# Layer B of a two-layer decoder: the norms of queries and keys, one chain for two token blocks in place of one for each

## The chip, the cores and the metric

One NeuronCore of a Trainium2 chip runs the whole program in one launch. The metric is device time in microseconds (us), and lower is better. The names of the engines in this document are those of the profile: PE is TensorE, DVE is VectorE, ACT is ScalarE, POOL is GpSimd, SP issues most of the DMAs.

## What is computed

The input x has 1024 tokens of 1024 columns, in float32; 16 learned meta tokens are put ahead of them. Layer A (stick-breaking attention and an MLP) comes first. Layer B has differential attention with 8 heads. Of each head it needs two queries and two keys of 64 columns and one value of 128 columns. Each query and key row is normalised and turned by position before the scores:

```python
kk = kv[..., :DIFF_HEADS * 2 * DIFF_QK_DIM].reshape(B, T, DIFF_HEADS, 2, DIFF_QK_DIM)
k1 = apply_partial_rope(rmsnorm(kk[..., 0, :], kv_k_norm_g[0]), cos, sin)
k2 = apply_partial_rope(rmsnorm(kk[..., 1, :], kv_k_norm_g[1]), cos, sin)
...
qq = (hn @ b_w_q[j]).reshape(B, T, DIFF_HEADS, 2, DIFF_QK_DIM)
q1 = apply_partial_rope(rmsnorm(qq[..., 0, :], b_q_norm_g[j, 0]), cos, sin)
q2 = apply_partial_rope(rmsnorm(qq[..., 1, :], b_q_norm_g[j, 1]), cos, sin)
o = differential_attention(q1, q2, k1, k2, vv, lam)
```

`rmsnorm(x, g)` is `x * rsqrt(mean(x * x) + EPS) * g`, here over 64 columns: one number for each token and each of the four rows (two queries, two keys).

## The kernel before

**Stages.** The program runs layer A's attention, its MLP, layer B's attention (the stretch from about 1399 to 2004 us of the span) and layer B's MLP. The change touches layer B's attention alone.

**Items of a head.** Tokens are handled in 8 blocks of 128 (b = 1 to 8); b = 0 is the 16 meta tokens. For head h and block b, `item(b)` makes the projection: 24 matmuls of 384 columns into a PSUM tile `bpj` (two buffers, tag `pj`), of which columns 0 to 255 are the four query and key rows of 64 and the last 128 are the value. ACT and DVE turn the value into the two halves `bv`. `rope_block` then takes the query and key part. ACT writes it to `raw` and its squares to `bsq`; DVE sums the squares to four numbers in `ss`, and scales them and adds EPS; `rsqrt` takes Ln on ACT, and `newton` takes Exp on ACT and then three small instructions on DVE (`na`, `na`, `ny`). Next DVE multiplies `raw` by `ny` into `kn`, POOL multiplies by the gains and does the rotation (six to ten instructions), ACT makes the first half of `hl` and DVE the second. For block 1 the two key rows of the meta tokens join: n = 6 columns in place of 4.

**Transposes.** `rope_stack(b)` turns `hl` by four PE transposes into a PSUM tile `bq`, which ACT copies into the head's `q` and `k` tiles. For heads 1 to 7 that tile has the tag `pj` too, so `bpj` and `bq` share two buffers, and they get them in the order of the program. `hl` and `kn` have two buffers each.

**Attention.** `b_unit(h, g)` makes scores (`sc_b`) of 256 queries against all keys so far, their maximum (`mxb`, DVE), exponentials (`eb`, `wb`, ACT) and the weighted difference (`wb`, DVE). `b_unit_av` transposes it (`ptb`, evacuated to `wtb` by ACT and DVE) and multiplies by the values (`avb`).

**What sets the order.** The code lists the items and transposes of head h + 1 in a stream that is fed between the pieces of head h's attention; the transpose of block b is listed DEFER = 3 blocks behind its projection. A scheduler then fixes the order of each engine's instructions when the program is built. Which engine does a copy (`evac`, `scopy`) is decided by running sums of estimated costs in `load`. On the chip each engine takes its instructions in that fixed order.

**Weights.** The first item of a head also loads its weights (`bws`, three buffers), scales them on POOL, and splits them on ACT (`bwh`) and DVE (`bwl`, 128x384, eight of them). They have nine buffers for eight pieces, so most of a head's splits wait until the last projection of the head ahead of it has read its own.

Of the kernel before, what the change touches and what calls it, by code (L numbers as in the profile page):

```python
# [8 lines left out]
F32 = mybir.dt.float32  # L9
F32R = mybir.dt.float32r  # L10
BF16 = mybir.dt.bfloat16
AF = mybir.ActivationFunctionType
ALU = mybir.AluOpType
# [65 lines left out]
def kernel(ctx: ExitStack, tc: tile.TileContext, inp, out):  # L79
# [23 lines left out]
    def act(o, i, func, **kw):  # L103
        load["a"] += 64 + 0.86 * fsize(o) + (93 if "bias" in kw else 0)
        nc.scalar.activation(out=o, in_=i, func=func, **kw)  # L105
# [5 lines left out]
    def tt(o, a, b, op):  # L111
        load["v"] += 60 + 1.04 * fsize(o)
        nc.vector.tensor_tensor(out=o, in0=a, in1=b, op=op)  # L113
# [1111 lines left out]
    with ExitStack() as st:  # L1225
# [28 lines left out]
        def rsqrt(v, n, tag, tg="n"):  # L1254

            y = sp.tile([P, 8], F32, tag=f"{tg}y", bufs=2, name=f"ny{tag}")[:, :n]
            a = sp.tile([P, 8], F32, tag=f"{tg}a", bufs=2, name=f"na{tag}")[:, :n]
            act(y, v, AF.Ln)
            newton(y, v, a)
            return y  # L1260

        def rope_block(h, b, ps, tm):

            tag = f"{h}_{b}"
            n = 6 if b == 1 else 4
            ss = sp.tile([P, 8], F32, tag="ss", bufs=2, name=f"ss{tag}")
            sq = sp.tile([P, 4, HD], F32, tag="sq", bufs=1, name=f"bsq{tag}")
            kn = sp.tile([P, 6, HD], F32, tag="kn", bufs=2, name=f"kn{tag}")
            raw = sp.tile([P, 4, HD], F32, tag="raw", bufs=2, name=f"raw{tag}")
# [3 lines left out]
            nc.vector.tensor_reduce(out=ss[:, 0:4], in_=sq, axis=AX.X, op=ALU.add)  # L1273
            if b == 1:
                nc.vector.memset(ss[:, 4:6], 1.0)
                nc.gpsimd.memset(kn[:, 4:6], 1.0)
                for m in range(2):
                    act(sq[:NM, m], tm[:, m * HD:(m + 1) * HD], AF.Square, accum_out=ss[:NM, 4 + m:5 + m])
            nc.vector.tensor_scalar(out=ss[:, :n], in0=ss[:, :n], scalar1=1.0 / HD, scalar2=EPS, op0=ALU.mult, op1=ALU.add)
            y = rsqrt(ss[:, :n], n, tag)  # L1280
            tt(kn[:, 0:4], raw, y[:, 0:4, None].to_broadcast([P, 4, HD]), ALU.mult)
            if b == 1:
                tt(kn[:NM, 4:6], tm[:, 0:P].rearrange("p (m d) -> p m d", d=HD), y[:NM, 4:6, None].to_broadcast([NM, 2, HD]), ALU.mult)
                ptt(kn[:, 4:6], kn[:, 4:6], gqk[:, 2:4], ALU.mult)
# [34 lines left out]
        def b_items(h):  # L1319
# [26 lines left out]
            def item(b):  # L1346
# [25 lines left out]
                st_[b] = rope_block(h, b, ps, st_["tm"])  # L1372
# [254 lines left out]
```

## Time and profile before

| what | us |
|---|---|
| median of 3 runs | 2743.18 |
| lowest and highest of them | 2738.76, 2744.81 |
| the profiled execution, its own time | 2740.28 |
| span of that execution, first to last instruction | 2738.5 |
| PE busy in it | 2613.1 |
| DVE busy | 1987.0 |
| ACT busy | 1508.1 |
| POOL busy | 318.1 |

The profile is of one execution, whose time lies 2.9 us below the median of the runs, and 1.8 us above its own span. Busy times are unions of an engine's instructions, so that two that overlap count once.

### The profile page before, as it was taken

Reading aid. Unit: us, or ns where it says so; the run is one execution under the profiler, and the core shown is the slowest. Engines: PE = TensorE matmul, PEld = TensorE weight load, DVE = VectorE, ACT = ScalarE, POOL = GpSimd, SP = SyncE. Lnnn points to the kernel's source line nnn. Section 1 sums busy time; section 2 is a strip of 40 time slices with the busy share of each in tenths; the row PEclk is TensorE's granted clock in tenths of the full one; section 3 lists DMA queues with packets and bytes.
Section 4 is the critical chain, followed back from the end, with each engine's and each line's share of the span. In section 5 each row is a group of like instructions: output and inputs, shape, how many; then the busy total and the mean of one; then the engine's idle time right before and its main releaser. Section 6 shows DMA issues by size and latency. Waiting matters only on the chain.

```text
span 2738.5 us, 49906 instructions
## 1 busy us (share of the span) xinstructions
PE 2613.1 (95%) x18271; PEld 2469.2 (90%) x18271; DVE 1987.0 (73%) x4009; ACT 1508.1 (55%) x3545; POOL 318.1 (12%) x708
## 2 busy tenths in 40 slices
PE   7999999989899999999989999999898999999999
PEld 7899898869899999999989899999897999987787
DVE  6998888897775665865767788888768666557645
ACT  4566666675355555344546667677545555544443
POOL 2211111000000000000024344443100000000000
PEclk9999999999999999999999999999999999999999
DMA  7333332345334446843431122223352444486343
GB/s 208 98 85 83 84 83 77 103 131 149 99 129 140 151 146 223 319 118 101 135 88 44 40 55 55 55 55 104 118 172 69 156 142 155 154 317 225 93 110 121
DMA packets 298711, 341.76 MB, mean 125 GB/s; under 512 B 32538, under 2 KB 209347, under 8 KB 298467
## 3 DMA queue, kind: packets, MB, share of 16 engines
q1 hardware_dynamic: 289106, 334.32, 39.4%
q10 hardware_dynamic: 9360, 4.26, 0.6%
q8 instruction: 144, 2.36, 0.4%
q14 instruction: 101, 0.82, 0.1%
HBM read 206.99 MB, written 97.28 MB: 111 GB/s over the span
## 4 chain that ended last, share of the span: by engine, by line
PE 74%; DVE 11%; DMA 4%; ACT 3%; issue 2%; POOL 1%; SPq 1%; DVEq 0%; ACTq 0%; POOLq 0%
PE mia L159 12%; PE mib L159 11%; PE moa L159 11%; PE mob L159 9%; PE bpj L159 8%; PE pj L159 6%; PE opb L159 2%; PE sc_b L159 2%; DVE kp L498 2%; PE av L159 2%; PE avb L159 2%; PE sc L159 2%; PE pt L162 1%; PE opa L159 1%; DMA bb<-u_d 1%
## 5 line engine op out<-in xcount | busy, mean ns | idle before, releaser
L159 PE MATMUL moa<-wba,waa 128*128 128x260 f32 x2688 | 325.3, 284 | 0.4 <-DVE wba L113 0.4
L159 PEld LDWEIGHTS moa<-wba,waa 128*128 128x128 f32 x2688 | 324.7, 189 | 0.6 <-DVE wba L113 0.6
L159 PE MATMUL mob<-wab,wbb 128*128 128x512 f32 x1344 | 313.8, 394 | 4.5 <-DVE hqb L113 2.8
L159 PEld LDWEIGHTS mob<-wab,wbb 128*128 128x128 f32 x1344 | 251.7, 188 | 65.6 <-issue 3.9
L159 PE MATMUL pj<-xa,wh 128*128 128x400 f32 (+2 forms) x1152 | 291.2, 332 | 6.1 <-DVE rsa L668 5.8
L159 PE MATMUL bpj<-bwh,xb 128*128 128x384 f32 x1024 | 285.7, 347 | 8.9 <-ACT k L99 5.4
L159 PEld LDWEIGHTS pj<-xa,wh 128*128 128x128 f32 x1152 | 202.2, 192 | 7.7 <-POOL ws L121 6.1
L159 PEld LDWEIGHTS bpj<-bwh,xb 128*128 128x128 f32 x1024 | 187.7, 190 | 13.7 <-ACT k L99 8.5
L498 DVE TENSOR_TENSOR_SCAN kp<-kp 128x144 f32<-128x144 f32 (+7 forms) x128 | 184.6, 1447 | 18.2 <-ACT kp L105 17.4
L159 PE MATMUL pj<-xa,wl 128*128 128x384 f32 (+2 forms) x576 | 189.8, 329 | 0.1
L159 PE MATMUL bpj<-bwl,xb 128*128 128x384 f32 x512 | 174.1, 340 | 0.0
L1338 POOL TENSOR_SCALAR bws<-bws,gains 128x128 f32<-128x128 f32 (+1 forms) x128 | 64.7, 511 | 832.8 <-DVE accx L113 776.9
L105 ACT ACTIVATE w<-sc,rsa 128x392 f32<-128x392 f32 (+4 forms) x224 | 121.2, 543 | 42.2 <-PE sc L159 40.4
L105 ACT ACTIVATE kp<-sc,rsa 128x392 f32<-128x392 f32 (+4 forms) x224 | 120.1, 538 | 15.6 <-DVE w L113 15.6
L1396 DVE TENSOR_REDUCE mxb<-sc_b 128x1 f32<-128x144 f32 (+6 forms) x224 | 109.3, 502 | 15.6 <-PE sc_b L159 14.0
L99 ACT CAST wt<-pt 128x512 fp32r<-128x512 f32 (+1 forms) x160 | 84.5, 546 | 61.2 <-PE av L159 45.3
L162 PE MATMUL pt<-cst,w 128*128 128x128 f32 x576 | 96.5, 279 | 21.0 <-DVE w L113 9.0
L113 DVE TENSOR_TENSOR wt<-pt,wt 128x512 fp32r<-128x512 f32 (+1 forms) x160 | 98.2, 628 | 19.7 <-ACT wt L99 18.9
L113 DVE TENSOR_TENSOR w<-w,kp 128x143 f32<-128x143 f32 (+7 forms) x128 | 110.9, 872 | 2.0
L159 PE MATMUL av<-wt,v 128*128 128x256 f32 (+1 forms) x640 | 105.3, 288 | 6.5 <-DVE wt L113 5.6
L159 PEld LDWEIGHTS pj<-xa,wl 128*128 128x128 f32 x576 | 110.0, 191 | 0.6 <-DVE wl L113 0.4
L159 PEld LDWEIGHTS av<-wt,v 128*128 128x128 f32 x640 | 90.2, 192 | 10.6 <-DVE wt L113 7.2
(484 smaller groups left out, 7417.3 us busy)
## 6 DMA issues: line engine op xcount, KB each, us to landing
ba<-u_d SPq DMA_DIRECT2D x112, 260.0 KB, 2.8
bb<-u_d SPq DMA_DIRECT2D x112, 256.0 KB, 2.7
mwsa<-in_mlp_w_in_dram SPq DMA_DIRECT2D x32, 512.0 KB, 3.9
mwsb<-in_mlp_w_in_dram SPq DMA_DIRECT2D x32, 512.0 KB, 3.9
o_d<-oh SPq DMA_DIRECT2D x52, 256.0 KB, 2.5
ws<-in_a_w_qkv_dram SPq DMA_DIRECT2D x24, 512.0 KB, 4.2
qb<-q SPq DMA_DIRECT2D x128, 64.0 KB, 2.0
a12a<-in_mlp_w_out_dram SPq DMA_DIRECT2D x16, 512.0 KB, 8.0
```

The lines of the kernel that those rows point to most:

```text
L99: nc.scalar.copy(out=o, in_=i)
L105: nc.scalar.activation(out=o, in_=i, func=func, **kw)
L113: nc.vector.tensor_tensor(out=o, in0=a, in1=b, op=op)
L159: return nc.tensor.matmul(o, lhsT=l, rhs=r, start=start, stop=stop, **kw)
L162: return nc.tensor.transpose(out=o, in_=i, identity=ident)
L498: nc.vector.tensor_tensor_scan(out=rv, data0=rv, data1=rv, initial=1.0, op0=ALU.mult, op1=ALU.bypass)
L1338: nc.gpsimd.tensor_scalar(out=ws[:, s], in0=ws[:, s], scalar1=gains[:, gc + k:gc + k + 1], scalar2=1.0, op0=ALU.mult, op1=ALU.mult)
L1396: nc.vector.tensor_reduce(out=mx[:, j:j + 1], in_=ps[:, 0], axis=AX.X, op=ALU.max, negate=True)
```

## The change

`rope_block` of an odd block now stops after its sum of squares and returns nothing; it leaves `ss` and `raw` in `prs`. `rope_block` of the even block behind it puts its own four sums beside them, and one chain (scale, Ln, Exp, `na`, `na`, `ny`) is run on 8 columns, or 10 for blocks 1 and 2 with the meta tokens' two. Then the new function `rope` is called twice, for the odd block and for the even one: it holds the multiplication by `ny`, the rotation and the making of `hl`, as they were. `raw` gets four buffers in place of two. The number of matmuls stays as it was; the built program has 125 DVE and 66 ACT instructions fewer.

```diff
@@ -1253,8 +1253,8 @@
 
         def rsqrt(v, n, tag, tg="n"):
 
-            y = sp.tile([P, 8], F32, tag=f"{tg}y", bufs=2, name=f"ny{tag}")[:, :n]
-            a = sp.tile([P, 8], F32, tag=f"{tg}a", bufs=2, name=f"na{tag}")[:, :n]
+            y = sp.tile([P, 10], F32, tag=f"{tg}y", bufs=2, name=f"ny{tag}")[:, :n]
+            a = sp.tile([P, 10], F32, tag=f"{tg}a", bufs=2, name=f"na{tag}")[:, :n]
             act(y, v, AF.Ln)
             newton(y, v, a)
             return y
@@ -1262,25 +1262,42 @@
         def rope_block(h, b, ps, tm):
 
             tag = f"{h}_{b}"
-            n = 6 if b == 1 else 4
-            ss = sp.tile([P, 8], F32, tag="ss", bufs=2, name=f"ss{tag}")
+            odd = b % 2
+            if odd:
+                prs["ss"] = sp.tile([P, 10], F32, tag="ss", bufs=2, name=f"ss{tag}")
+            ss = prs["ss"]
             sq = sp.tile([P, 4, HD], F32, tag="sq", bufs=1, name=f"bsq{tag}")
-            kn = sp.tile([P, 6, HD], F32, tag="kn", bufs=2, name=f"kn{tag}")
-            raw = sp.tile([P, 4, HD], F32, tag="raw", bufs=2, name=f"raw{tag}")
+            raw = sp.tile([P, 4, HD], F32, tag="raw", bufs=4, name=f"raw{tag}")
             evac(raw.rearrange("p m d -> p (m d)"), ps[:, 0:2 * P], scale=rsx[:, b:b + 1])
             act(sq, raw, AF.Square)
             load["v"] += 60 + 1.04 * 4 * HD
-            nc.vector.tensor_reduce(out=ss[:, 0:4], in_=sq, axis=AX.X, op=ALU.add)
+            o = 2 if odd else 6
+            nc.vector.tensor_reduce(out=ss[:, o:o + 4], in_=sq, axis=AX.X, op=ALU.add)
             if b == 1:
-                nc.vector.memset(ss[:, 4:6], 1.0)
+                nc.vector.memset(ss[:, 0:2], 1.0)
+                for m in range(2):
+                    act(sq[:NM, m], tm[:, m * HD:(m + 1) * HD], AF.Square, accum_out=ss[:NM, m:m + 1])
+            if odd:
+                prs["raw"] = raw
+                return []
+            v = ss[:, 0 if b == 2 else 2:10]
+            n = v.shape[1]
+            nc.vector.tensor_scalar(out=v, in0=v, scalar1=1.0 / HD, scalar2=EPS, op0=ALU.mult, op1=ALU.add)
+            y = rsqrt(v, n, tag)
+            return [rope(h, b - 1, prs["raw"], y[:, n - 8:n - 4], y[:, 0:2], tm), rope(h, b, raw, y[:, n - 4:n], None, tm)]
+
+        prs = {}
+
+        def rope(h, b, raw, y, ym, tm):
+
+            tag = f"{h}_{b}"
+            n = 6 if b == 1 else 4
+            kn = sp.tile([P, 6, HD], F32, tag="kn", bufs=2, name=f"kn{tag}")
+            if b == 1:
                 nc.gpsimd.memset(kn[:, 4:6], 1.0)
-                for m in range(2):
-                    act(sq[:NM, m], tm[:, m * HD:(m + 1) * HD], AF.Square, accum_out=ss[:NM, 4 + m:5 + m])
-            nc.vector.tensor_scalar(out=ss[:, :n], in0=ss[:, :n], scalar1=1.0 / HD, scalar2=EPS, op0=ALU.mult, op1=ALU.add)
-            y = rsqrt(ss[:, :n], n, tag)
-            tt(kn[:, 0:4], raw, y[:, 0:4, None].to_broadcast([P, 4, HD]), ALU.mult)
+            tt(kn[:, 0:4], raw, y[:, :, None].to_broadcast([P, 4, HD]), ALU.mult)
             if b == 1:
-                tt(kn[:NM, 4:6], tm[:, 0:P].rearrange("p (m d) -> p m d", d=HD), y[:NM, 4:6, None].to_broadcast([NM, 2, HD]), ALU.mult)
+                tt(kn[:NM, 4:6], tm[:, 0:P].rearrange("p (m d) -> p m d", d=HD), ym[:NM, :, None].to_broadcast([NM, 2, HD]), ALU.mult)
                 ptt(kn[:, 4:6], kn[:, 4:6], gqk[:, 2:4], ALU.mult)
             ptt(kn[:, 0:4], kn[:, 0:4], gqk, ALU.mult)
             t0 = 0 if b == 1 else b
@@ -1369,7 +1386,8 @@
                 r = rsx[:, b:b + 1]
                 acopy(d["v"][:, b, 0, :], ps[:, 2 * P:], scale=r)
                 stt(d["v"][:, b, 1, :], ps[:, 2 * P:], r, f(d["v"][:, b, 0, :]), ALU.mult, ALU.subtract)
-                st_[b] = rope_block(h, b, ps, st_["tm"])
+                for x, hl in zip((b - 1, b), rope_block(h, b, ps, st_["tm"])):
+                    st_[x] = hl
 
             return item, lambda b: rope_stack(d, h, b, st_[b])
```

Where instructions stand now. In the names below the first number is the head and the second the block (`ny5_2`: head 5, block 2), for `sc_b`, `mxb` and `avb` the second is the unit g; the last number is the buffer's own.

VectorE at the start of head 5, before: the chain of block 1 ends here, and that of block 2 begins.

```order
L113 TENSOR_TENSOR na5_1_22455<-ny5_1_22454 128x6
L1396 TENSOR_REDUCE mxb4_2_0_22324<-sc_b4_2_0_1_328_22341 128x1
L117 SCALAR_TENSOR_TENSOR na5_1_22455<-na5_1_22455,ss5_1_22442 128x6
L1396 TENSOR_REDUCE mxb4_2_1_22355<-sc_b4_2_1_0_0_22356 128x1
L1398 TENSOR_TENSOR mxb4_2_0_22324<-mxb4_2_0_22324 128x1
L117 SCALAR_TENSOR_TENSOR ny5_1_22454<-na5_1_22455,ny5_1_22454 128x6
L1273 TENSOR_REDUCE ss5_2_22516<-bsq5_2_22517 128x4
L109 COPY os3_21553<-psq3_3_22411 128x2
L113 TENSOR_TENSOR kn5_1_22444<-raw5_1_22445,ny5_1_22454 128x256
L113 TENSOR_TENSOR kn5_1_22444<-tm5_22306,ny5_1_22454 16x128
L1279 TENSOR_SCALAR ss5_2_22516<-ss5_2_22516 128x4
```

The same place of the changed kernel, on VectorE:

```order
L113 TENSOR_TENSOR na5_2_22312<-ny5_2_22311 128x10
L1416 TENSOR_TENSOR mxb4_2_1_22175<-mxb4_2_1_22175 128x1
L113 TENSOR_TENSOR wtb4_1_1_22457<-ptb4_1_1_22453,wtb4_1_1_22457 128x384
L117 SCALAR_TENSOR_TENSOR na5_2_22312<-na5_2_22312,ss5_1_22262 128x10
L117 SCALAR_TENSOR_TENSOR ny5_2_22311<-na5_2_22312,ny5_2_22311 128x10
L113 TENSOR_TENSOR kn5_1_22318<-raw5_1_22264,ny5_2_22311 128x256
L113 TENSOR_TENSOR kn5_1_22318<-tm5_22126,ny5_2_22311 16x128
L113 TENSOR_TENSOR kn5_2_22341<-raw5_2_22306,ny5_2_22311 128x256
L1427 TENSOR_TENSOR s04_20945<-mxb4_2_1_22175 128x1
L117 SCALAR_TENSOR_TENSOR bv5_22027<-bpj5_3_22498,rsx_81,bv5_22027 128x128
```

One chain of 10 columns (`128x10`) now serves both blocks, and the two multiplications into `kn5_1` and `kn5_2` stand one behind the other, with the meta tokens' between them.

VectorE at the end of head 5, before: block 8's chain ends, and block 7, whose chain stood further up, gets its `hl`.

```order
L113 TENSOR_TENSOR na5_8_23256<-ny5_8_23255 128x4
L117 SCALAR_TENSOR_TENSOR wb5_1_23120<-eb5_1_0_23134,mxb5_1_0_23121,wb5_1_23120 128x400
L117 SCALAR_TENSOR_TENSOR na5_8_23256<-na5_8_23256,ss5_8_23247 128x4
L1409 TENSOR_TENSOR s05_22208<-mxb5_1_1_23139 128x1
L117 SCALAR_TENSOR_TENSOR ny5_8_23255<-na5_8_23256,ny5_8_23255 128x4
L113 TENSOR_TENSOR hl5_7_23107<-kn5_7_23082,hl5_7_23107 128x4x64
L113 TENSOR_TENSOR kn5_8_23249<-raw5_8_23250,ny5_8_23255 128x256
```

The same chain of the changed kernel, on VectorE:

```order
L113 TENSOR_TENSOR na5_8_23023<-ny5_8_23022 128x8
L1427 TENSOR_TENSOR s05_22028<-mxb5_1_1_22908 128x1
L113 TENSOR_TENSOR bwl6_7_23187<-bws6_7_23182,bwh6_7_23186 128x384
L117 SCALAR_TENSOR_TENSOR na5_8_23023<-na5_8_23023,ss5_7_22873 128x8
L117 SCALAR_TENSOR_TENSOR ny5_8_23022<-na5_8_23023,ny5_8_23022 128x8
L113 TENSOR_TENSOR kn5_7_23029<-raw5_7_22875,ny5_8_23022 128x256
L113 TENSOR_TENSOR kn5_8_23045<-raw5_8_23017,ny5_8_23022 128x256
```

Block 7's multiplication into `kn5_7` now waits for block 8's chain, and its `hl5_7` comes 19 rows behind the last of these. Counted over the whole order, from the instruction that reads block 8's projection (`bv`) to `hl` of block 7 there are, for heads 1 to 6, 30, 25, 34, 40, 34, 37 DVE rows before, and 62, 47, 45, 52, 51, 42 now. On TensorE, from the last matmul of block 8's projection to the first transpose of block 7, there are 89, 120, 110, 120, 110, 117 matmuls before, and 127, 125, 129, 131, 124, 115 now.

TensorE where head 1 ends and head 2 begins, before: the transposes of head 1's block 7 (`bq1_7`) and the first projection of head 2 (`bpj2_1`).

```order
L159 MATMUL bpj2_0_19013<-bwl2_6_18998,xm_17056 48x256
L159 MATMUL bpj2_0_19013<-bwh2_7_19007,xm_17056 48x256
L159 MATMUL avb0_3_18710<-wtb0_3_3_18815,bv0_17068 128x256 x2
L159 MATMUL avb0_3_18710<-wtb0_3_3_18815,bv0_17068 128x128 x3
L159 MATMUL psq0_2_18841<-ones_66,osqb0_2_18523 128x2 x2
L159 MATMUL sc_b1_1_1_1_0_18693<-k1_17772,q1_1_17774 128x264
L159 MATMUL sc_b1_1_1_1_0_18693<-k1_17772,qbb1_1_18657 128x264
L162 MATMUL bq1_7_19058<-idr_62,hl1_7_18647 128x128 x4
L159 MATMUL bpj2_0_19013<-bwl2_7_19008,xm_17056 48x256
L159 MATMUL bpj2_1_19065<-bwh2_0_18937,xb0_16177 128x384
```

The same place of the changed kernel, on TensorE:

```order
L159 MATMUL sc_b1_2_0_1_328_18801<-idb_64 128x128
L159 MATMUL sc_b1_2_1_0_0_18816<-k1_17736,q1_2_17739 128x392
L159 MATMUL sc_b1_2_1_0_0_18816<-k1_17736,qbb1_2_18780 128x392
L159 MATMUL avb1_0_18846<-wtb1_0_0_18851,bv1_17741 128x256 x2
L159 MATMUL avb1_0_18846<-wtb1_0_0_18851,bv1_17741 128x128 x3
L159 MATMUL psq0_3_18982<-ones_66,osqb0_3_18767 128x2 x2
L159 MATMUL avb1_0_18846<-bzm0_17053,bvm1_17055 128x256 x2
L162 MATMUL ptb1_1_0_19117<-cst_60,wb1_1_18573 128x128 x4
L162 MATMUL bq1_7_18986<-idr_62,hl1_7_18713 128x128 x4
L159 MATMUL bpj2_1_18993<-bwh2_0_18865,xb0_16177 128x384
```

The transposes still stand directly ahead of head 2's projections. But the matmuls that stand there without a projection between them are now 79 (all of attention, or `bq1_7`), where the longest such run in the middle of the stage was 41 before.

## Rows read from the trace of the kernel before

**Rows 1.** The page, part 1: busy us, share, instructions by engine.
```profile
PE 2613.1 (95%) x18271; PEld 2469.2 (90%) x18271; DVE 1987.0 (73%) x4009; ACT 1508.1 (55%) x3545; POOL 318.1 (12%) x708
```

**Rows 2.** Busy time by stretch: heading, and the whole stage.
```profile
core 0: us, PE busy (x) PEld busy (x) DVE busy (x) ACT busy (x) POOL busy (x), PEclk, DMA share, GB/s
1399.00:2004.00 605.00, 572.42 (x3797) 535.64 (x3796) 475.00 (x1583) 395.31 (x1331) 226.76 (x636) 0.98 0.24 68
```

**Rows 3.** Busy time by stretch: first and last of six boundaries, and sum.
```profile
1518.00:1550.20 32.20, 30.36 (x205) 27.59 (x204) 26.57 (x92) 22.33 (x78) 15.91 (x43) 1.00 0.23 61
...
1860.00:1893.20 33.20, 31.87 (x224) 29.90 (x225) 31.29 (x104) 24.40 (x86) 15.08 (x41) 1.00 0.27 73
sum 185.10, PE 179.08 PEld 168.21 DVE 168.69 ACT 135.45 POOL 95.31; mean PE 29.85 PEld 28.03 DVE 28.12 ACT 22.58 POOL 15.89
```

**Rows 4.** Busy time by stretch: sum of six middles between them.
```profile
sum 231.80, PE 223.82 PEld 209.52 DVE 175.80 ACT 154.30 POOL 71.97; mean PE 37.30 PEld 34.92 DVE 29.30 ACT 25.72 POOL 12.00
```

**Rows 5.** Waits of TensorE, 1446 to 1940: total us, times, longest.
```profile
PE bpj L159 <- ACT k L99: 6.5, 15, 1.1
PE avb L159 <- DVE wtb L113: 2.4, 5, 0.8
PE sc_b L159 <- ACT eb L105: 2.1, 3, 0.9
```

**Rows 6.** Groups by line and shape, 1399 to 2004: the merged instructions.
```profile
L105 ACT ACTIVATE ny<-ss 128x4 f32<-128x4 f32 x56 | 12.0, 214 | 13.7 <-DVE ss L1279 13.7
...
L1279 DVE TENSOR_SCALAR ss<-ss 128x4 f32<-128x4 f32 x56 | 11.1, 198 | 0.8
...
L113 DVE TENSOR_TENSOR na<-ny 128x4 f32<-128x4 f32 x56 | 9.7, 174 | 4.3 <-ACT ny L105 3.9
...
L117 DVE SCALAR_TENSOR_TENSOR na<-na,ss 128x4 f32<-128x4 f32 x56 | 9.2, 163 | 0.6
...
L117 DVE SCALAR_TENSOR_TENSOR ny<-na,ny 128x4 f32<-128x4 f32 x56 | 8.8, 158 | 0.8
```

**Rows 7.** VectorE in order of time, in a boundary: start, us.
```profile
1754.34 0.15 DVE L113 TENSOR_TENSOR nao<-nyo 128x8 f32<-128x8 f32 x1
1754.45 0.16 DVE L117 SCALAR_TENSOR_TENSOR na<-na,ss 128x4 f32<-128x4 f32 x1
1754.53 0.16 DVE L117 SCALAR_TENSOR_TENSOR nao<-nao,os 128x8 f32<-128x8 f32 x1
1754.65 0.16 DVE L117 SCALAR_TENSOR_TENSOR ny<-na,ny 128x4 f32<-128x4 f32 x1
1754.73 0.26 DVE L117 SCALAR_TENSOR_TENSOR nyo<-nao,nyo 128x8 f32<-128x8 f32 x1
1754.91 0.41 DVE L113 TENSOR_TENSOR kn<-raw,ny 128x256 f32<-128x256 f32 x1
1755.25 0.55 DVE L1396 TENSOR_REDUCE mxb<-sc_b 128x1 f32<-128x392 f32 x1
```

**Rows 8.** VectorE in order of time, head 0, block 1.
```profile
1424.74 0.17 DVE L117 SCALAR_TENSOR_TENSOR na<-na,ss 128x6 f32<-128x6 f32 x1
1424.94 0.17 DVE L117 SCALAR_TENSOR_TENSOR ny<-na,ny 128x6 f32<-128x6 f32 x1
```

**Rows 9.** VectorE in order of time: block 7, heads 1, 4, 5.
```profile
1527.64 0.41 DVE L113 TENSOR_TENSOR hl<-kn,hl 128x256 fp32r<-128x256 f32 x1
...
1737.79 0.63 DVE L113 TENSOR_TENSOR hl<-kn,hl 128x256 fp32r<-128x256 f32 x1
...
1806.41 0.43 DVE L113 TENSOR_TENSOR hl<-kn,hl 128x256 fp32r<-128x256 f32 x1 [0.99 <-ACT hl L144]
```

**Rows 10.** TensorE in order of time: the transposes of those blocks.
```profile
1528.33 0.46 PE L162 MATMUL bq<-idr,hl 128*128 128x128 f32 x4
...
1741.33 0.51 PE L162 MATMUL bq<-idr,hl 128*128 128x128 f32 x4
...
1807.71 0.54 PE L162 MATMUL bq<-idr,hl 128*128 128x128 f32 x4
```

## The prediction

> **What bounds the kernel now.** I read the page first. PE is busy for 95% of the span, DVE for 73%, ACT for 55% [rows 1]. The change removes no matmul, so the question is where in layer B's attention, the 605 us from 1399 to 2004, PE is held up by DVE or ACT. Over that stage PE is busy for 572.4 us and DVE for 475.0 [rows 2], which looks like PE's stage. Cut in pieces it is two things. I took the time at which DVE finishes `bv` of block 8 of a head and of block 3 of the next, for heads 1 to 6. In these six boundaries, 185.1 us together, DVE is busy for 168.7, or 91% [rows 3]; this is where the next head's eight `bwl` come on top. In the six middles between them, 231.8 us, DVE is busy for 175.8, or 76%, and PE for 223.8, or 97% [rows 4]. So what leaves DVE can be worth something in the boundaries, and is hidden by PE's projections in the middles. The waits of PE from 1446 to 1940 us give the ceiling of what can be won where PE shows as idle: the three largest are 6.5 us for `k` from ACT, 2.4 for `wtb` from DVE and 2.1 for `eb` from ACT [rows 5]. None is for the tiles that the change touches.
>
> **The change part by part.**
>
> *Merged instructions.* 64 chains become 32. On DVE that is 32 x 4 = 128 instructions fewer (the order shows 125, as a few copies change engine), on ACT 64 fewer (66 in the order). Their mean durations are 198, 174, 163 and 158 ns on DVE and some 210 on ACT [rows 6], so the busy times should fall by up to 32 x 0.69 = 22 us on DVE and 32 x 0.42 = 13.5 on ACT. Columns hardly cost: 4 to 10 of them are far below what such an instruction takes. But the time that matters is from start to start. In a boundary, with an independent instruction behind it, `na` holds DVE for 1754.53 - 1754.45 = 0.08 us and `ny` for the same [rows 7]. With the next of its own chain directly behind it, it holds DVE for 1424.94 - 1424.74 = 0.20 us [rows 8]. Counted over the order, 82 chain instructions stand in the six boundaries now and 46 after, 36 fewer; pairs of dependents that are direct neighbours there rise from 10 to 16, since fewer chains leave less to put between. The gain in the boundaries is then 36 x 0.10 - 6 x 0.12 = 2.9 us. The bounds are 36 x 0.08 - 0.7 = 2.2 and, by full durations, 36 x 0.17 = 6.2. I take 2.9, since rows 7 are from a boundary and rows 6 count overlaps. In the middles and in head 0 I take 0: PE covers it.
>
> The Trainium skill, page "Perfetto Trace Analysis", section "Optimizing Scalar/DVE Operations", puts DVE's overhead per instruction at about 60 ns on SBUF and says that grouping helps if the engine is saturated. By that figure the boundaries would give 36 x 0.06 = 2.2 us (an estimate from that page), the lower of my bounds; rows 7 agree with it nearly.
>
> *Moved work.* The odd block's multiplication into `kn`, its rotation on POOL (a gain product, four products, two sums; more for block 1), `hl` on ACT and DVE, and four transposes now come behind the even block's squares. On DVE, 3 `kn` and 3 `hl` fewer stand in the six boundaries (21 each before, 18 now); they move to the middles. At 1755.25 - 1754.91 = 0.34 us each [rows 7] that is 2.0 us, between 0 (if the next boundary pays) and 6 x 0.43 = 2.6. On POOL two rotations now run one after the other; POOL is busy for 95.3 of 185.1 us there [rows 3], so half of it is free, and I cost this at 0. If POOL were late, `hl` would be, and its price is that of the next paragraph. SP's queue gets its q copies for the scores later by a place or two; they are read two blocks on. 0.
>
> *A later block 7.* The transposes of block b stand three items behind its projection. For blocks 1, 3 and 5 the odd block loses one item of three, some 24 matmuls. Block 7 is tight already: in head 1 its `hl` ends at 1528.05 and PE takes it at 1528.33, in head 4 1738.42 and 1741.33, in head 5 1806.84 and 1807.71, so 0.3, 2.9 and 0.9 us to spare [rows 9, 10] (hl of block 7 is the (8h + 7)th on DVE). Behind it on PE stand the next head's projections, which share its PSUM buffers. In the changed order `hl` of block 7 stands 32, 22, 11, 12, 17 and 5 DVE rows further behind block 8's `bv` in heads 1 to 6, at some 0.33 us a row (33.2 us for 104 [rows 3]): 10.6, 7.3, 3.6, 4.0, 5.6 and 1.7 us. PE comes to it 38, 5, 19, 11, 14 and -2 matmuls later, at 33.2/224 = 0.15 us: 5.7, 0.8, 2.9, 1.7, 2.1, -0.3. With head 4's 2.9 us to spare where I have no row, PE would wait 4.6 us in head 1, 3.6 in head 2, 2.6 in head 5 and 0 elsewhere: up to 11 us. Most of it comes back: the rows that come in between are the next attention's scores done early, and over the six boundaries DVE's rows fall from 567 to 519. I take 1.0, of 0 to 11.
>
> *ACT.* The waits for `k` are for ACT, which loses 13.5 of 395 us [rows 2]: 3% of 6.5 us, so 0.2; at most half of it, 3.2.
>
> *The sum.* -2.9 - 2.0 + 1.0 - 0.2 = -4.1 us. The profiled execution took 2740.3 itself (a span of 2738.5 and 1.8 around it) and would be at 2736.2. It lies 2.9 below the median of the runs, 2743.2, so a median of runs should be near **2739 us**. That is 0.15% less; 0.2%, or 5.5 us, is about what a measurement of this kernel can tell from no change.
>
> **The rivals.**
>
> *Faster beyond that.* The boundaries are so full that DVE's durations count whole: 6.2 + 2.6, and ACT gives the 3.2: -12, so 2731. For it: DVE at 91% there; the last boundary took 33.2 us for 31.3 us of DVE work [rows 3]. Against it: PE is at 97% in the same stretches (179.1 of 185.1), so that its own matmuls follow close behind. It decides from 1.4 us more than the sum.
>
> *Slower.* Block 7 late, with nothing given back: PE stops at `bq` ahead of the next head's projections. With 11 in place of 1.0 the sum is +6, so 2749; with POOL's two rotations in a row late by another 0.5 us in seven heads, 2753. For it: 0.3 us to spare in head 1, and 79 matmuls without a projection between them there. Against it: DVE has 48 rows less to do over the six boundaries. It decides from some 10 us of new waits of PE for `hl`. The Trainium skill's same section also says that where ScalarE and VectorE are not saturated but cause bubbles elsewhere, breaking instructions up may finish work sooner; that speaks against joining two blocks, and would be this case.
>
> *Nothing happens.* PE paces the whole stage, and the freed time turns into DVE idle time: 2743. This lies inside the forecast's case.
>
> **How the numbers follow.** I give the forecast's case, a time within 0.2% (2737.7 to 2748.7, of which I hold 2737.7 to 2743 the likelier part), 0.40; faster 0.37; slower 0.23, of which some 0.05 is for a new order that falls out badly at several places at once. The forecast is 2739. The low end is the faster case with the upper ends of its terms and the scatter of the runs (2743.2 - 2738.8 = 4.4 below their median): 2731 - 4 = 2727. The high end is the slower case, 2752. I leave out about 1 in 10 at either end.
>
> **What would show it.** Right: DVE busy falls by 13 to 22 us from 1987 and ACT by some 13 from 1508; PE busy stays within a few us; in the boundaries DVE falls below 90%, and their sum shrinks by 2 to 6 us; the middles do not get shorter. Wrong towards slower: `PE bq` or `PE bpj` waits for `DVE hl` or `ACT k` by several us, above all at the end of heads 1, 2 and 5. Wrong towards faster: the middles shrink too, which would mean that ACT or DVE paced PE there in small waits that the idle time does not show.

## The result, and the profile after

The changed kernel takes 2768.98 us (median of 4 runs, 2768.02 to 2777.48); beside it, the kernel before took 2743.73. The ratio is 1.0098, 95% interval 1.0083 to 1.0113: 25 us slower, where 4 us faster was forecast. The profiled execution is the one of 2768.02.

The page, part 1, of the changed kernel (compare [rows 1]):

```profile
PE 2632.9 (95%) x18271; PEld 2486.4 (90%) x18271; DVE 1973.9 (71%) x3884; ACT 1498.5 (54%) x3478; POOL 321.7 (12%) x708
```

DVE lost 13.1 us of work and ACT 9.6, as they should. PE, which has the same 18271 matmuls, is busy 19.8 us longer. To see where, I cut layer B's attention from its first projection to the first matmul of the output product. Busy time by stretch (columns as in [rows 2]), the kernel before:

```profile
1409.60:2004.60 595.00, 567.64 (x3763) 531.08 (x3763) 467.11 (x1543) 387.78 (x1302) 222.27 (x625) 0.98 0.24 67
```

Of its six boundaries, [rows 3] has the first, the last and the sum; the four between are:

```profile
1589.40:1621.60 32.20, 31.28 (x221) 29.35 (x222) 29.83 (x102) 24.21 (x84) 16.01 (x42) 1.00 0.27 74
1659.00:1686.60 27.60, 27.29 (x196) 26.18 (x196) 25.18 (x88) 20.83 (x72) 15.61 (x41) 1.00 0.29 79
1725.40:1757.60 32.20, 31.14 (x220) 29.03 (x220) 30.48 (x101) 22.86 (x82) 17.60 (x47) 1.00 0.26 73
1795.50:1823.20 27.70, 27.14 (x196) 26.16 (x195) 25.34 (x87) 20.83 (x73) 15.10 (x41) 1.00 0.29 79
```

The changed kernel: the same cut, the six boundaries (from block 8's `bv` of a head to block 3's of the next, as in [rows 3]) with their sum, and the sum of the six middles (as in [rows 4]):

```profile
1413.30:2033.70 620.40, 582.68 (x3762) 543.17 (x3763) 454.72 (x1418) 377.43 (x1235) 225.65 (x625) 0.96 0.23 65
...
1520.20:1565.60 45.40, 40.45 (x251) 36.72 (x252) 32.81 (x107) 27.00 (x94) 12.86 (x29) 0.92 0.16 41
1604.70:1636.40 31.70, 29.75 (x188) 27.16 (x188) 24.21 (x78) 20.22 (x72) 11.05 (x28) 0.95 0.25 66
1671.30:1708.60 37.30, 34.56 (x225) 31.89 (x225) 27.07 (x84) 22.92 (x77) 21.91 (x58) 0.95 0.24 67
1743.80:1778.00 34.20, 32.12 (x224) 29.69 (x224) 29.52 (x94) 22.81 (x78) 12.89 (x31) 1.00 0.26 73
1813.30:1849.60 36.30, 33.48 (x211) 30.84 (x210) 27.24 (x84) 23.31 (x80) 14.98 (x37) 0.91 0.25 70
1888.80:1917.80 29.00, 27.64 (x193) 25.99 (x192) 23.95 (x78) 20.09 (x70) 7.15 (x20) 1.00 0.25 72
sum 213.90, PE 198.00 PEld 182.30 DVE 164.81 ACT 136.36 POOL 80.84; mean PE 33.00 PEld 30.38 DVE 27.47 ACT 22.73 POOL 13.47
...
sum 232.00, PE 222.79 PEld 210.45 DVE 175.21 ACT 150.88 POOL 88.83; mean PE 37.13 PEld 35.08 DVE 29.20 ACT 25.15 POOL 14.81
```

The stage grew from 595.0 to 620.4 us, 25.4 of the 27.7 us between the two profiled executions (2740.28 and 2768.02). Of these 25.4 us PE is idle for 10.4 more (37.7 in place of 27.4) and busy for 15.0 more with the same matmuls. The second part is mostly the granted clock, 0.96 for 0.98 (some 11 us, by the estimate in the last section). The place is as clear: the boundaries take 213.9 us, not 185.1, and the middles 232.0, not 231.8. The heads can't be compared by these lengths alone, because the cut follows DVE's `bv` and holds another number of matmuls now (251 for 205 in head 1, 188 for 221 in head 2, 1292 for 1262 in all six). By the matmul, heads 1, 2, 3 and 5 carry the loss: 0.181, 0.169, 0.166 and 0.172 us for each, where it was 0.157, 0.146, 0.141 and 0.141. Heads 4 and 6 went from 0.146 to 0.153 and from 0.148 to 0.150. The clock is below 1.00 in the rows of those four heads and of no other: 0.92, 0.95, 0.95 and 0.91.

Waits of TensorE in the changed kernel, over the same part as [rows 5] (total us, times, longest):

```profile
PE sc_b L159 <- ACT wb L105: 4.8, 7, 1.5
PE sc_b L159 <- ACT eb L105: 3.3, 3, 2.2
PE avb L159 <- ACT wtb L99: 3.0, 6, 1.0
PE ptb L162 <- DVE bob L113: 2.6, 2, 2.2
PE bq L162 <- DVE hl L113: 2.4, 3, 1.2
PE avb L159 <- DVE wtb L113: 2.0, 5, 0.9
...
PE bpj L159 <- ACT k L99: 1.0, 3, 0.5
```

No single wait stands out. The one for `hl`, by which the prediction would have known the slower rival, is 2.4 us, and the wait for `k` of [rows 5] fell from 6.5 to 1.0. PE loses its time in many small waits for attention's own steps.

The end of head 1 shows how. TensorE in order of time, the changed kernel:

```profile
1527.64 0.28 PE L159 MATMUL bpj<-bwl,xm 128*48 128x256 f32 x1
...
1532.24 0.39 PE L159 MATMUL sc_b<-k,q 128*128 128x264 f32 x1 [0.92 <-ACT wb L105]
...
1536.16 0.51 PE L159 MATMUL avb<-bzm,bvm 128*128 128x256 f32 x2 [0.95 <-DVE bzm L113]
...
1538.34 0.39 PE L159 MATMUL avb<-wtb,bv 128*128 128x256 f32 x1 [0.35 <-ACT wtb L99]
1540.24 0.42 PE L159 MATMUL sc_b<-k,q 128*128 128x328 f32 x1 [1.52 <-ACT wb L105]
...
1544.26 0.81 PE L162 MATMUL bq<-idr,hl 128*128 128x128 f32 x4
1544.88 0.65 PE L159 MATMUL bpj<-bwh,xb 128*128 128x384 f32 x1
```

VectorE, the same place:

```profile
1519.90 0.34 DVE L117 SCALAR_TENSOR_TENSOR bv<-bpj,rsx,bv 128x128 fp32r<-128x128 f32 x1
...
1541.15 0.42 DVE L113 TENSOR_TENSOR hl<-kn,hl 128x256 fp32r<-128x256 f32 x1
```

The last projection matmul ahead of the gap is at 1527.64 and the next at 1544.88. In between PE does 79 matmuls of attention and `bq`, among them head 1's `bq` of block 7 at 1544.26, directly ahead of head 2's block 1 (`bpj2_1`). `hl` of block 7 was done at 1541.57, so PE did not wait for it here. It came later still: in the order fixed at the build, 75 matmuls of attention stand between the last projection and `bq` 7, they wait for ACT and DVE at several steps, and from 1541.2 us on they run at the lower clock. Three stretches of it by busy time (the whole gap; and within it the last of the idling and what follows):

```profile
1528.00:1544.90 16.90, 13.03 (x84) 11.71 (x84) 14.72 (x51) 10.05 (x36) 8.82 (x23) 0.89 0.13 36
1534.40:1541.20 6.80, 3.98 (x27) 3.15 (x26) 5.61 (x18) 4.19 (x15) 5.19 (x16) 1.00 0.02 6
1541.20:1548.00 6.80, 6.80 (x31) 6.80 (x30) 4.50 (x16) 2.93 (x11) 0.20 (x1) 0.50 0.00 0
```

Over the gap PE is busy for 13.03 of 16.90 us and DVE for 14.72. From 1541.2 us on PE idles no more, and from 1544.88 it has projections again, but at a granted clock of 0.50, the lower of its two levels (1.2 GHz): a 384-column matmul starts 0.32 us behind the one before it, where it is 0.18 at the upper level a few us later:

```profile
1545.32 0.52 PE L159 MATMUL bpj<-bwl,xb 128*128 128x384 f32 x1
1545.64 0.84 PE L159 MATMUL bpj<-bwh,xb 128*128 128x384 f32 x2
...
1548.65 0.34 PE L159 MATMUL bpj<-bwl,xb 128*128 128x384 f32 x1
1548.83 0.34 PE L159 MATMUL sc_b<-k,q 128*128 128x392 f32 x1
```

Why the gap is there is seen in the program's order. On PE, other matmuls between the four of `bq` 7 (a head's block 7) and the nearest matmul of a projection, for heads 1 to 6 (the last three kernels are experiments, below):

| kernel | ahead of `bq` 7 | behind it | the projection behind it |
|---|---|---|---|
| before | 9, 21, 2, 21, 2, 19 | 0, 16, 5, 14, 3, 16 | block 0 (head 1), 2 |
| changed | 75, 31, 4, 19, 17, 11 | 0, 0, 4, 0, 0, 0 | block 1 (head 1), 2 |
| e5 | 29, 24, 4, 20, 14, 11 | 0, 0, 4, 0, 4, 3 | block 1 (head 1), 2 |
| e14 | 75, 27, 19, 17, 24, 20 | 0, 0, 0, 0, 0, 0 | block 1 (head 1), 2 |
| e9 | 53, 0, 9, 15, 0, 3 | 5, 23, 18, 18, 25, 17 | block 2 (head 1), 3 |

In the changed kernel a projection of the next head stands right behind `bq` 7 in five heads of six. `bq` and `bpj` share two PSUM buffers and get them in the order of the code. The code lists block 7's transposes ahead of that projection, and for heads 1 to 7 these tiles begin on PE in the same sequence in both orders: the scheduler did not move a projection past them. They come late because block 7 now waits for block 8.

The table does not tell the heads apart: head 3, with four matmuls between, is among the slower ones, and heads 4 and 6, with none, are not. Nor does the place alone cost anything. In e8 (below) the numbers behind `bq` 7 are 0, 3, 10, 1, 1, 0, its block 7 does not wait for block 8, and its +2 us can't be told from nothing.

### The profile page after: what moved, and what is told of

The parts are those of the page before. It is cut to its first block, busy times and chain, and to the rows that moved or that the text cites. A ratio compares the mean times of both kernels' runs of the same rounds, so it can differ in the third digit from the quotient of the medians.

```text
span 2766.2 us, 49724 instructions
## 1 busy us (share of the span) xinstructions
PE 2632.9 (95%) x18271; PEld 2486.4 (90%) x18271; DVE 1973.9 (71%) x3884; ACT 1498.5 (54%) x3478; POOL 321.7 (12%) x708
## 4 chain that ended last, share of the span: by engine, by line
PE 73%; DVE 12%; DMA 4%; ACT 3%; issue 2%; POOL 1%; SPq 0%; DVEq 0%; ACTq 0%; POOLq 0%
PE mia L159 11%; PE mib L159 11%; PE moa L159 10%; PE mob L159 10%; PE bpj L159 8%; PE pj L159 6%; PE opb L159 2%; DVE kp L498 2%; PE av L159 2%; PE sc_b L159 2%; PE avb L159 2%; PE opa L159 2%; PE sc L159 1%; PE pt L162 1%; PE ofa L159 1%
```

## Experiments

The kernels below are made from one with a list of the blocks that are the first of a pair; with (1, 3, 5, 7) its order is that of the changed kernel, and with none that of the kernel before, though `raw` has four buffers and the small tiles ten columns. So these two parts of the change do nothing to the order.

| run | what it is | us, median | ratio to before, 95% interval |
|---|---|---|---|
| e1_pairs_not_78 | pairs (1,2) (3,4) (5,6) | 2756.22 | 1.0042 (1.0027 to 1.0056) |
| e2_pair_78_only | pair (7,8) | 2750.91 | 1.0022 (1.0012 to 1.0031) |
| e3_moved_apart | code listed as changed, chains apart | 2742.91 | 0.9992 (0.9977 to 1.0008) |
| e4_pairs_23_45_67 | pairs (2,3) (4,5) (6,7) | 2776.46 | 1.0115 (1.0090 to 1.0139) |
| e5_joint_scale_apart | one joint scale, rest of the chains apart | 2761.92 | 1.0072 (1.0052 to 1.0091) |
| e6_pairs_defer4 | changed, DEFER = 4 | 2761.72 | 1.0070 (1.0052 to 1.0087) |
| e7_before_defer4 | before, DEFER = 4 | 2750.41 | 1.0025 (1.0015 to 1.0035) |
| e8_before_early12 | before, head 1's list a little earlier | 2746.08 | 1.0005 (0.9994 to 1.0016) |
| e9_pairs_odd_later | changed, odd blocks' `bq` listed later | **2739.45** | 0.9981 (0.9967 to 0.9996) |
| e10_before_odd_later | before, the same listing | 2744.91 | 1.0004 (0.9994 to 1.0013) |
| e11_pair_12_only | pair (1,2) | 2752.98 | 1.0027 (1.0014 to 1.0041) |
| e12_pair_56_only | pair (5,6) | 2744.45 | 1.0001 (0.9987 to 1.0014) |
| e13_pairs_only7_later | changed, block 7's `bq` alone later | 2741.85 | 0.9997 (0.9985 to 1.0010) |
| e14_pairs_135_later | changed, `bq` of 1, 3, 5 later, 7 not | 2764.60 | 1.0074 (1.0058 to 1.0090) |
| e15_joint_scale_odd_later | e5 with the listing of e9 | 2746.77 | 1.0012 (1.0002 to 1.0023) |
| e16_pairs_234567_later | e4, first blocks' `bq` later | 2763.81 | 1.0080 (1.0063 to 1.0097) |
| e17_pair_78_later | e2, block 7's `bq` later | **2736.65** | 0.9975 (0.9964 to 0.9985) |

**Which pairs.** My first theory was A: the late block 7 is the whole cost. The rivals were B, the long runs of PE without a projection that the order forms, and C, that each delayed odd block costs alike.

```diff
+FIRST = (1, 3, 5)
...
-            odd = b % 2
-            if odd:
+            first, second = b in FIRST, b - 1 in FIRST
+            if not second:
```

A block in no pair has its own chain, as before. The other runs have FIRST = (7,), (2, 4, 6), (1,) and (5,).

e1: 

> Blocks 1 to 6 in pairs as in the change, 7 and 8 each with a chain of its own as before. The change lost 25 us. Theory A, a late block 7 at the end of each head: the loss is gone, +0 to +5 us to the kernel before. Theory B, the loss follows the runs of matmuls without a projection that the new order happens to form (here 58 at the longest, at the start of head 3; 79, 59 and 54 in the change): +8 to +12. Theory C, every delayed odd block costs alike: three quarters of it, +19.

e2: 

> Only blocks 7 and 8 share a chain, 1 to 6 have their own as before. Theory A: the whole loss, +18 to +25 us. Theory B (longest runs 46 and 40, against 41 and 39 before): +0 to +6. Theory C: one quarter, +6.

e4: 

> Pairs 2 and 3, 4 and 5, 6 and 7; blocks 1 and 8 alone. Block 7 is now the later one of its pair and is not held back; 96 DVE instructions fewer than before. Theory A: no loss, -4 to +2 us. Theory B (longest run 36): -4 to +2. Theory C: three quarters, +19.

e1 came out at +11.2 us and e2 at +5.9, 17 together, not 25. A had e2 at +18 to 25: it fell in that form. B had both (8 to 12, and 0 to 6); C had e2, but e1 at +19. B had e4 at most +2, and it was +31, the slowest of all: B fell as well, as did A again, since block 7 does not wait in it. C had it at +19, 12 too few. Two single pairs came later:

e11: 

> Only blocks 1 and 2 are joined. In the kernel before, block 1 has 6.7 to 9.6 us between its finished parts and its transposes in heads 1 to 7. Theory S (a pair costs only where the odd block has little to spare, that is 7 and, less, 3): -2 to +3 us. Theory C (every pair costs alike, a fourth of the whole change): +4 to +9 us.

e12: 

> Only blocks 5 and 6 are joined. In the kernel before, block 5 has 8 to 12.6 us to spare, the most of all. Theory S: -2 to +3 us. Theory C: +4 to +9 us.

Pair (5,6) costs nothing, by theory S; (1,2) costs 9, by C. What a pair costs does not follow from one number for each pair.

**The wait or the merging.** e3 lists both blocks' work behind the even block's squares, as the changed code does, but keeps two chains (`chain` is the scaling and `rsqrt`):

```diff
-            y = rsqrt(v, n, tag)
-            return [rope(h, b - 1, prs["raw"], y[:, n - 8:n - 4], y[:, 0:2], tm), rope(h, b, raw, y[:, n - 4:n], None, tm)]
...
+                y = chain(ss[:, 0 if b == 2 else 2:6], f"{h}_{b - 1}")
+                n = y.shape[1]
+                odd = rope(h, b - 1, prs["raw"], y[:, n - 4:n], y[:, 0:2], tm)
+                return {b - 1: odd, b: rope(h, b, raw, chain(ss[:, 6:10], tag), None, tm)}
```

e3: 

> All four pairs as in the change, and the odd block's chain and rotation wait for the even block's squares as there, but the two chains stay separate, 128 DVE and 64 ACT instructions more than the change. Theory A: the loss of the change and the price of the instructions, +25 to +30 us. Theory B (longest run 34): +0 to +3. Theory C: +25 or more.

2742.91, the same as before. This does not refute the wait. Nothing ties the odd chain to the even squares here, and the scheduler put it back ahead of them (on DVE the chain of `ss5_7` stands ahead of `bv5_8` again). It shows that the new listing by itself costs nothing. e5 ties them by one instruction (against e3):

```diff
-                y = chain(ss[:, 0 if b == 2 else 2:6], f"{h}_{b - 1}")
-                n = y.shape[1]
+                v = ss[:, 0 if b == 2 else 2:10]
+                nc.vector.tensor_scalar(out=v, in0=v, scalar1=1.0 / HD, scalar2=EPS, op0=ALU.mult, op1=ALU.add)
+                u = ss[:, 0 if b == 2 else 2:6]
+                n = u.shape[1]
+                y = rsqrt(u, n, f"{h}_{b - 1}")
...
-                return {b - 1: odd, b: rope(h, b, raw, chain(ss[:, 6:10], tag), None, tm)}
+                return {b - 1: odd, b: rope(h, b, raw, rsqrt(ss[:, 6:10], 4, tag), None, tm)}
```

e5: 

> Both blocks of a pair are scaled by one instruction of 8 or 10 columns, so the odd block waits for the even one's squares as in the change; Ln, Exp, na, na and ny are again made once for each block (4 or 6 columns). Theory W (the wait for the second block's squares is the cost, in whichever way the chains are formed): +18 to +28 us against the kernel before, and at least ten stretches of lowered clock in layer B's attention. Theory M (the joint chain itself, with the order that the scheduler forms from it, is the cost; the wait is not): within 6 us of the kernel before.

+17.8 us, the low end of theory W's range: the wait costs 18 of the 25 where only the scaling is merged. `bq` 7 again stands right ahead of a projection, with 0 to 4 matmuls between them (table above). Its stage by busy time:

```profile
1416.10:2027.10 611.00, 580.12 (x3763) 540.76 (x3763) 459.94 (x1511) 381.07 (x1302) 221.32 (x625) 0.97 0.23 65
```

PE is idle for 30.9 us, only 3.5 more than before, and busy for 12.5 more, with the clock at 0.97. Its stage has six stretches at half clock, where theory W wanted ten, though they last as long in sum (42.3 us, against 43.6 in the changed kernel). The wait it is, but W's number of stretches was off.

**Only a fragile order?** e8 is the kernel before with EARLY = 0.12 in place of 0.1.

e8: 

> How much the time hangs on the order alone: the kernel before, with head 1's list set 0.02 of a head earlier; no instruction is added or removed, but the scheduler's order changes at many places. Theory L (a tuned order was lost; any change of the order costs some 10 us or more): +8 to +25 us. Theories W, M and D: within 5 us of the kernel before.

+2 us, less than can be told from nothing. So a shifted order need not cost 10 us; that another one does is not excluded by this one run.

**The time that the transposes have.** e6 and e7 set DEFER = 4 in place of 3, with and without the change.

e6: 

> The change, with the transposes listed four items behind their projection in place of three. To be read against the kernel before with the same four. Theory D (the odd block only lacks one item of time, and PE stops at its transposes): the pairs cost at most 5 us more than the control. Theory W in its other form (the cost is in the stretches where no projection stands on PE and DVE must first finish the pair's chain; the deadline of the transposes does not matter): 12 us or more over the control, and the longest run of matmuls without a projection (75 here) shows PE idle and a lowered clock behind it.

e7: 

> The control: the kernel before, with the transposes listed four items behind. All theories: 0 to +6 us against the kernel before (longest runs of matmuls without a projection 46, 46, 44 against 41, 39, 39). If it is slower by 12 us or more, an order with four is itself bad, and the run with pairs and four tells nothing.

The control lost 6.3 us, a little above its range, and the pairs 17.6: 11 us between them, in place of 25. That lies between the two theories and tells only that the place of the transposes matters. Theory W's other sign did not come: the run of 75 matmuls without a projection takes from 1528.08 to 1539.79 us, PE is busy for 10.4 of these 11.7, and no lowered clock follows. So a long run does not by itself cost what it costs in the changed kernel. e9 moves the transposes of the odd blocks alone (1, 3, 5 and 7), and e10 does the same to the kernel before (the line is e10's; e9 has `b in FIRST`, which names the same blocks):

```diff
-                        for b in range(9) for late in (0, DEFER) if b or not late)
+                        for b in range(9) for late in (0, DEFER + 0.9 * (b % 2)) if b or not late)
```

e9: 

> The change, with the transposes of odd blocks alone listed 0.9 items later (just ahead of the even one's). Theory D (what the odd block lacks is the time between its projection and its transposes): at most 8 us more than its control below. Theory W2 (the longer chain costs wherever attention stands on PE without a projection, and the deadline is not what counts): 14 us or more over the control.

e10: 

> The control: the kernel before, one chain for each block, with the same later listing of the odd blocks' transposes. All theories: -3 to +5 us against the kernel before.

e9 takes 2739.45 us: the loss is gone, and the change is 5.5 us faster than its control and 4.3 faster than the kernel before. Busy time by stretch in e9: the stage, the six boundaries' sum, the six middles' sum, and the end of head 1 to head 2's first `bv`:

```profile
1414.40:2004.90 590.50, 566.05 (x3762) 530.39 (x3763) 450.52 (x1418) 376.27 (x1235) 223.80 (x625) 0.99 0.24 68
...
sum 188.60, PE 181.04 PEld 170.00 DVE 159.57 ACT 132.30 POOL 85.30; mean PE 30.17 PEld 28.33 DVE 26.60 ACT 22.05 POOL 14.22
...
sum 222.90, PE 219.57 PEld 207.41 DVE 169.32 ACT 147.39 POOL 80.22; mean PE 36.59 PEld 34.57 DVE 28.22 ACT 24.56 POOL 13.37
...
1520.20:1539.40 19.20, 17.93 (x133) 16.44 (x133) 17.71 (x59) 13.10 (x45) 11.23 (x28) 1.00 0.31 80
```

The last of these is 32.5 us in the changed kernel, and 19.9 in the kernel before:

```profile
1520.20:1552.70 32.50, 27.55 (x172) 24.58 (x173) 25.40 (x84) 20.20 (x71) 12.86 (x29) 0.89 0.18 48
...
1518.00:1537.90 19.90, 18.41 (x131) 15.98 (x129) 16.50 (x56) 13.41 (x44) 12.66 (x31) 1.00 0.31 85
```

TensorE in e9, the same place:

```profile
1525.67 0.36 PE L162 MATMUL bpj<-bwh,xb 128*128 128x384 f32 x1
...
1530.71 0.42 PE L162 MATMUL bpj<-bwh,xb 128*128 128x384 f32 x1
...
1534.47 0.39 PE L162 MATMUL sc_b<-k,q 128*128 128x264 f32 x1 [0.92 <-ACT wb L108]
...
1538.62 0.54 PE L165 MATMUL bq<-idr,hl 128*128 128x128 f32 x4
1540.62 0.38 PE L162 MATMUL avb<-wtb,bv 128*128 128x256 f32 x1 [1.46 <-ACT wtb L102]
```

VectorE in e9:

```profile
1538.12 0.44 DVE L116 TENSOR_TENSOR hl<-kn,hl 128x256 fp32r<-128x256 f32 x1 [0.39 <-ACT hl L147]
...
1539.02 0.34 DVE L120 SCALAR_TENSOR_TENSOR bv<-bpj,rsx,bv 128x128 fp32r<-128x128 f32 x1
```

This is the picture on which I rest the cause. `hl` of block 7 is done at 1538.56, nearly as late as in the changed kernel (18.4 us behind block 8's `bv`, which ends at 1520.21, against 21.3). But head 2's block 1 no longer stands behind it. Its projection fills PE from 1525.67 on, between the pieces of attention, and the clock stays at 1.00. The idle 0.92 us ahead of 1534.47 did not lower it, nor did the 1.46 ahead of 1540.62. A run of 62 matmuls without a projection stays around `bq` 7 (53, the four and 5, by the table), and the loss is gone all the same.

**Which odd block.** Listed 0.9 items later, block 7's transposes move behind one more projection of the next head, as the table above shows, and those of block 5 behind its short first one (block 0, the meta tokens); those of blocks 1 and 3 stay between the same two projections, a little further down in the attention. So I parted them:

e13: 

> The change, with block 7's transposes alone listed 0.9 items later, which puts them behind the next head's first projections in place of ahead of them. Theory A2 (the cost is block 7's transposes standing ahead of the next head's projections): -8 to +3 us against the kernel before. Theory D2 (each odd block lacks time): +8 to +18 us.

e14: 

> The change, with the transposes of blocks 1, 3 and 5 listed 0.9 items later and block 7's left where they were (runs of 79 and 54 matmuls without a projection ahead of heads 2's items stay). Theory A2: +18 to +30 us. Theory D2: +3 to +14 us.

e13 (with `b == 7` in the diff above) is at 2741.85, e14 (`b in (1, 3, 5)`) at 2764.60. So in the changed kernel it is block 7, which theory A had, by what stands behind its transposes, which A had left out. Where no block waits, the same listing is worth nothing (e10, +1.2). What this does not explain is e1: there the other three pairs cost 11 us without a block 7 that waits, and in e13, with the same three pairs, nothing of it is left. In e14 the same end of head 1 takes as long as in the changed kernel, and the clock falls as there:

```profile
1520.60:1553.20 32.60, 27.66 (x171) 24.51 (x172) 25.57 (x84) 20.32 (x70) 12.85 (x29) 0.90 0.18 48
```

e17 does it to the pair (7,8) alone, e16 to the pairs of e4.

e17: 

> Only blocks 7 and 8 joined, block 7's transposes listed 0.9 items later. Theory A3: -4 to +2 us against the kernel before (the pair alone cost +6 where they stood). If +5 us or more stay, block 7's transposes are not what the pair cost.

e16: 

> Blocks 2 and 3, 4 and 5, 6 and 7 joined, with the transposes of 2, 4 and 6 listed 0.9 items later; those of block 6 then stand ahead of most of the next head's block 1 no more. Theory A3 (in general: transposes of a waiting block that stand ahead of the next head's projections): -6 to +6 us against the kernel before. If +20 us or more stay, these pairs cost for another reason, which stays open.

e17 is the fastest kernel of this study, 2736.65 us, 6.9 below the kernel before, where +6 stood without the listing. e16 stays at +20 of 31. There block 6 is the first of the last pair, and in e4 a projection of the next head stood right behind its `bq` in four heads of six (0, 0, 7, 4, 0, 0 matmuls between). In e16 these are 1, 9, 19, 19, 19, 14, and most of the loss is still there: theory A3 does not hold for these pairs. Why these pairs cost 20 us more is open, and so are the 9 us of e11 and the 11 of e1.

**What the merging is worth.** e15 has the wait and the listing of e9 but separate Ln, Exp and Newton steps.

e15: 

> One instruction scales both blocks, so that the odd one waits for the even one's squares; the rest of the chain once for each block; odd blocks' transposes listed 0.9 items later. If the gain of the change with the later listing comes from the merged Ln, Exp, na, na and ny (DVE has some 96 instructions more here than with them joined), this takes 2742 to 2748 us, 3 to 8 more than it. If the gain is the new order's, the two are within 2 us.

2746.77 us, 7.3 more than e9; by the ratios, each to the kernel before in its own series, 0.0031 of 2744, or 8.5. So the merged steps do bring time, once nothing stands in their way; part of it may be the order that differs with them.

## Why the prediction was wrong

**What bounds the stage: right, but half of it.** PE paces the middles, which kept their length to 0.2 us. In the boundaries DVE was called the limit, and its work there fell from 168.69 to 164.81 us, 3.9 less, where 4.9 were forecast. Its share is 77% now, below the 90% that I had named as a good sign, but because the boundaries grew.

**Merged instructions and moved work: the busy times about right, the total by luck.** 13.1 us less DVE time in all (13 to 22 forecast), 9.6 on ACT (13 forecast). The merged forms take what the narrow ones did in [rows 6]. Groups by line and shape, the changed kernel:

```profile
L105 ACT ACTIVATE ny<-ss 128x8 f32<-128x8 f32 x24 | 5.4, 224 | 5.3 <-DVE ss L1285 5.2
...
L1285 DVE TENSOR_SCALAR ss<-ss 128x8 f32<-128x8 f32 x24 | 4.2, 175 | 0.2
...
L113 DVE TENSOR_TENSOR na<-ny 128x8 f32<-128x8 f32 x24 | 4.0, 166 | 2.5 <-ACT ny L105 2.4
...
L117 DVE SCALAR_TENSOR_TENSOR ny<-na,ny 128x8 f32<-128x8 f32 x24 | 3.9, 162 | 0.3
```

With the transposes listed later, the change is worth -4.3 us, where -4.1 was the sum and -5.1 the sum without the later block 7. Where the gain falls is another matter. The boundaries' cut of e9 is 188.6 us, longer than [rows 3]. Against e10 it is the same. Busy time by stretch in e10, the six boundaries' sum and the six middles':

```profile
sum 188.80, PE 181.01 PEld 170.99 DVE 164.05 ACT 132.32 POOL 93.59; mean PE 30.17 PEld 28.50 DVE 27.34 ACT 22.05 POOL 15.60
...
sum 225.90, PE 221.66 PEld 208.21 DVE 179.02 ACT 154.23 POOL 71.06; mean PE 36.94 PEld 34.70 DVE 29.84 ACT 25.71 POOL 11.84
```

DVE has 4.5 us less in e9's boundaries, near the 4.9 of the two terms, and they take 0.2 us less. It is the middles that are shorter, by 3.0 us, though I had put 0 there. And by e15 against e9 the merged steps, with the order that comes with them, are worth 7.3 us, where I had 2.9 and at most 6.2; the wait with the new listing then still costs 3.7 (e15 against the kernel before), for which I had 1.0. So neither the places nor the sizes of the terms are borne out, and that the total agrees is luck.

**A later block 7: the step that failed.** I took 1.0 us of 0 to 11 and wrote that most of it comes back; e13 measures 27 (2768.98 against 2741.85). The first half of the working held. I had `hl` of block 7 10.6 us later in head 1, and it is 11.3 (21.3 us behind block 8's `bv` in place of 10.0), though 33.2 us for 104 rows are 0.32 a row and not 0.33. The price was wrong in three ways, which the runs show:

- *Priced as a wait for `hl`.* I set DVE's delay against PE's arrival, at 0.15 us a matmul. PE came later than that: 84 matmuls in 16.90 us are 0.20 each, and DVE is busy for 14.72 of them: here, without projections, attention goes at the pace of DVE and ACT. So the waits carry other names (`wb`, `eb`, `wtb`), and the sign that I gave for this rival, 10 us of waits for `hl`, did not come. What is lost is the overlap of projections with attention, and that is not bounded by PE's wait for `hl`: the boundaries grew by 28.8 us, where I gave 11 at most.
- *"Most of it comes back".* I counted the scores done early as time gained for later, but the projections that PE kept for later came in one piece, and DVE, busy for 14.72 of 16.90 us in the gap of head 1, is busy for 4.50 of 6.80 at its end and behind it (1541.2 to 1548.0). The middles gave back nothing.
- *No term for the clock.* 15.0 of the 25.4 us are PE busier with the same matmuls. I had read the clock of the stage, 0.98 in [rows 2], as given.

The stage's +25.4 us is +28.8 in the boundaries, +0.2 in the middles and -3.6 in the rest (the first head and the tail). Some 4 us of this only moved: the boundaries' cuts hold 30 matmuls more and the rest 27 fewer.

**The rivals.** *Slower* had the place and the cause: block 7 late, nothing given back, 79 matmuls without a projection, two shared buffers. It had 2749 to 2753, and a chance of 0.23. e13 shows the place (one block's transposes listed later are worth 27 us, 2741.85 against 2768.98, and those of the three others 4, by e14), e5 that the wait is enough (18 us). Its price lacked the lost overlap and the clock. The Trainium skill's page "Perfetto Trace Analysis", section "Optimizing Scalar/DVE Operations", says that where ScalarE and VectorE are not saturated but cause bubbles on other engines, breaking instructions up may let work be done sooner. That joining was a loss here agrees with it in part: DVE is busy for 73% of the span, but it was busy for 91% of the boundaries [rows 3], where the loss fell. Also e5, whose instructions are broken up again all but one, still loses 18 us, and e9 shows that the joint instructions can stay if the consumer's place is moved: 2739.45 us against 2768.98. *Faster beyond that* and *nothing happens* fell with the result.

**What stays open.** e1, e4, e11 and e16: four pairings that cost 9 to 31 us without a block 7 that waits for 8. In their stages PE is idle for 33.3, 41.1, 30.3 and 36.6 us (27.4 before) and busy for 574.6, 583.8, 572.5 and 570.6 (567.6 before), so the loss has the same two parts, but what makes PE's gaps there was not found. That their orders merely fall out badly is not excluded. Nor is it shown why e1 and e2 give 17 us together and the change 25. Nor was it tried to give `bq` PSUM buffers of its own.

## What to carry to other kernels

When a change makes a value ready later, ask not only whether its consumer waits, but what is queued behind the consumer: here four small transposes, listed ahead of the next projections in two shared buffers, kept 24 large matmuls from filling PE. A delay at a place where one kind of work is the filler for another costs the overlap, which can be several times the wait that the profile names (25.4 us here, with 2.4 of waits for `hl`). If the gain is real, move the consumer in the listing together with the producer: one number in one line turned +25 us into -4.

## What the runs showed of the hardware

The granted clock fell to 0.50 for 43.6 us in ten stretches of the changed kernel's stage (first projection to first output matmul), and for 18.5 us in three in the kernel before. With 0.32 us a matmul there for 0.18 otherwise, 25.1 us more of it cost some 11 (25.1 x 0.14/0.32, an estimate), not far from half of the loss; 20.5 of the 43.6 us lie in the boundaries of heads 1, 2, 3 and 5, where the kernel before has none. The 11 are rough, since kernels that lose nothing differ in this too (7.1 us in e3, 27.1 in e8, one execution each). The stretches follow idle times of PE, as the one of 1.52 us ahead of 1540.24 above, but not each of them: e9 has 0.92 and 1.46 us of idling in the same place, and its clock stays at 1.00 to the end of the boundary (1555.5). So an idle us of PE can cost more than itself, and the list of waits does not show that part: it appears as PE being busy.
